# Diffusion backbone on one core: v of the gated-MLP quads in a slot of its own, normalised by ScalarE, and even gated blocks made one quad later

## The chip, the core and the metric

The kernel runs on 1 core of one Trainium2 chip. The core has TensorE (PE: matmuls; its weight loads have rows of their own, PEld), VectorE (DVE), ScalarE (ACT), GpSimd (POOL) and SyncE (SP), whose queue issues nearly all DMA transfers here. The metric is the device time of one execution in microseconds; of several runs the median is taken. The profile shown comes from one profiled execution.

## The reference, cut to what matters

Two layers are computed on 512 latent tokens of width 1024: a retention layer, then a gated MLP (gMLP) layer with spatial mixing over chunks of 128 tokens, and a final RMS norm. The change is in the gMLP layer:

```python
def gmlp_chunk_mixer(h, w_in, vnorm_g, w_s, b_s, w_out):
    u = h @ w_in[:, :GM_WIDTH]
    v = (h @ w_in[:, GM_WIDTH:2 * GM_WIDTH]).astype(F32)
    z = h @ w_in[:, 2 * GM_WIDTH:]
    v = v - jnp.mean(v, axis=-1, keepdims=True)
    v = v * lax.rsqrt(jnp.mean(v * v, axis=-1, keepdims=True) + NORM_EPS) * vnorm_g.astype(F32)
    b, l, w = v.shape
    vg = v.reshape(b, l // CHUNK, CHUNK, GM_GROUPS, w // GM_GROUPS)
    mixed = jnp.einsum('gij,bnjgc->bnigc', w_s.astype(F32), vg) + b_s.astype(F32).T[:, :, None]
    y = u * mixed.reshape(b, l, w).astype(u.dtype)
    return (y * jax.nn.silu(z)) @ w_out
```

GM_WIDTH is 2048 and GM_GROUPS is 8, so a group has 256 channels.

## The kernel before, in words

**Number format.** A float32 product is made of three matmuls in the format fp32r: each operand is split into a high part (a cast, by ScalarE) and a low part (the operand less its high part, by VectorE). `split` issues these two; `mm3` issues the three matmuls. A weight block of 128x1024 is fetched from DRAM by two DMAs of 256 KB into one of 7 slots (the tiles named `raw`), and its high and low parts stand in one of 4 `hl` tiles, used in turn. Those are freed when TensorE has finished the product that reads them.

**Quads.** Eight quads of u and z follow each other (`for i in range(UZ)`, quads 0 to 7). In quad i, 256 columns of u and z are computed for all 512 tokens, by Strassen's scheme for a 2x2 block product with 7 products instead of 8. The products stand in the order B11, T1, T2, B21, T3, B22, T4. The weights of T1 to T4 are combinations of two raw blocks, which VectorE makes in place (rows `raw<-raw`): T1 and T2 both rework the block 11, so the sum for T2 can be made only when the low part of T1 exists. Each product is 24 matmuls of 256 columns (rows `pst<-oA,hl` and `pst<-oS,hl`; the oA and oS tiles are the activations' splits). B11, T2, T3 and T4 add into one PSUM bank, x; B21 has a bank y, T1 and B22 a bank z. Between products that add into x, ScalarE copies its state out (rows `snap<-pst`: after B11, T1 and T2), and VectorE adds such copies to a bank to get the blocks 11, 12 and 22 of the result (rows `snap<-pst,snap`). The block 21 stays in x. Left blocks are the even feature block 2i, right ones the odd feature block 2i+1 (columns: 256 wide, u in the first half and z in the second).

**The spatial product and the gate.** v has been computed before the quads and spilled to DRAM. `load_vt(i)` fetches the 512 KB of v for group i in two halves and normalises each with two `tensor_scalar` on VectorE (v minus mean, times the reciprocal deviation). It is called after T2 of quad i-1, from a pool of eleven 2 KB buffers (`t2`). Behind B22 of quad i stand 16 matmuls of 128 columns (rows `pst<-wsT,vt`), 8 for each of two PSUM banks, `pms[0]` and `pms[1]`. T4 closes the quad. `gate_f(f, ...)` makes the gated block y of feature block f: SiLU of z by ScalarE (rows `yz`), then VectorE: one `scalar_tensor_tensor` from the spatial bank, two products with u, one with the SiLU, and the split of the result (rows `ya`; `yb` and `yc` are the same for other tiles). The odd block's gate stands after the spatial product, the even block's after T4.

**The output projection.** After quads 2, 4, 6 and at the end, `out1` multiplies four finished feature blocks with the output weights (rows `pst<-hl,ya`, 512 columns each): after quad 2 those of quads 0 and 1, and so on. Quads 1, 2, 4 and 6 follow another quad directly; quads 3, 5 and 7 follow an `out1`.

**What sets the order.** TensorE's order is that of the text. In this part of the kernel VectorE, ScalarE and SyncE are not held to the text: the framework's scheduler orders each of these queues when the program is built, and each engine then runs its own queue strictly in that order. All tile sizes and addresses are laid out ahead (`lay`); the slots `w0` to `w6` are the raw slots here, and `w7` and `la` are free in the quads of the kernel before.

Most rows of the profile bear line 54, the helper through which instructions are issued, so work is told apart by tile names.

Of the kernel before, what the change touches and what calls it, by code (L numbers as in the profile page):

```python
# [9 lines left out]
AF = mybir.ActivationFunctionType  # L10
ALU = mybir.AluOpType
AX = mybir.AxisListType

P = 128
# [5 lines left out]
NT = SEQ // P  # L20
# [6 lines left out]
HS = 256  # L27
# [40 lines left out]
def hybrid_kernel(ctx, tc, xT_d, cT_d, cv_d, sv_d, rows_d, ada0_d, adag_d, w_d, rope_d, dec_d, ws_d, id_d, out_d):  # L68
    nc = tc.nc
    pe, act, dve, sp = (Queue(tc, e) for e in (nc.tensor, nc.scalar, nc.vector, nc.sync))  # L70
# [11 lines left out]
    def st(shape, tag, dt=F32, bufs=1, name=None):  # L82
        return sb.tile(shape, dt, tag=tag, name=name or tag, bufs=bufs)

    T2 = 11
# [32 lines left out]
    def t2(name, shape=(P, 512), dt=F32):  # L118
        return st(list(shape), "t2", dt, bufs=T2, name=name)

    def pt(shape=(P, 512), tag="ps"):
        return ps.tile(list(shape), F32, tag=tag, name="pst", bufs=6 if tag == "ps" else 2)

    mm = pe.matmul
# [19 lines left out]
    def load(dst, src):  # L144
        sp.dma_start(dst, src)
# [147 lines left out]
    UZ = 8  # L293
# [781 lines left out]
    vt_d = [dram.tile([P, NT, HS], F32, name=f"vt{i}", tag=f"vt{i}") for i in range(8)]  # L1075
# [137 lines left out]
    wsT = st([P, D], "dec", name="wsT")  # L1213
# [4 lines left out]
    mv = st([P, NT, 2], "mv")  # L1218
    for t in range(NT):
        dve.bn_aggr(mv[:, t, :], bns[:, t, :, :])  # L1220
    rv = st([P, NT], "rv")
    act.activation(rv, mv[:, :, 1], AF.Sqrt, bias=eps, scale=1.0)
    dve.reciprocal(rv, rv)

    o1 = [st([P, D], f"s{t}", name="o1") for t in range(NT)]
    ya = st([P, 4, 2, SEQ], "hc", F32R, name="ya")
# [4 lines left out]
    def yf(f):  # L1231
        return ys[f % 6] if f < 14 else late_y[f - 14]

    def out1(p, hfs=range(2)):
        for hf in hfs:
            ws = [Q.get() for _ in range(2)]
            for t in range(NT):
                last = (p, hf, t) == (3, 1, NT - 1)
                for c in range(2 if last else 1):
                    n = HS if last else 512  # L1240
                    pr = pt((P, n))
                    for k in range(4):
                        y = yf(4 * p + k)
                        w = ws[k // 2][:, :, k % 2 * 512 + c * n:k % 2 * 512 + c * n + n]
                        mm3(pr, (y[:, 0, t * P:t * P + P], y[:, 1, t * P:t * P + P]), (w[:, 0, :], w[:, 1, :]), k == 0, k == 3)
                    if last:
                        last_part(t, c, pr)
                    else:
                        drain(p, t, hf, pr)
# [55 lines left out]
    vts = {}  # L1305

    def load_vt(i):
        vts[i] = []
        for th in range(2):
            v = t2("vt", (P, 2, HS))  # L1310
            load(v, vt_d[i][:, 2 * th:2 * th + 2, :])
            for t in range(2):
                n = 2 * th + t
                dve.tensor_scalar(v[:, t, :], v[:, t, :], mv[:, n, 0:1], rv[:, n:n + 1], ALU.subtract, ALU.mult)
            vts[i].append(v)

    def gate_f(f, pm, mine):

        g = f // 2
        a = t2("ya")  # L1320
        z1 = t2("yz")
        bb = bsb[:, g * P:g * P + P].unsqueeze(1).to_broadcast([P, NT, P])
        for th in range(2):
            act.activation(z1[:, th * HS:th * HS + HS], mine[th][:, HS:], AF.Silu)
        dve.scalar_tensor_tensor(a.rearrange("p (n i) -> p n i", n=NT), pm.rearrange("p (n i) -> p n i", n=NT),
                                 vg[:, f:f + 1], bb, ALU.mult, ALU.add)
        for th in range(2):
            h = a[:, th * HS:th * HS + HS]
            dve.tensor_tensor(h, mine[th][:, 0:HS], h, ALU.mult)
        dve.tensor_tensor(a, a, z1, ALU.mult)  # L1330
        y = yf(f)
        split((y[:, 0, :], y[:, 1, :]), a)

    load_vt(0)
    for i in range(UZ):
        got, pms = {}, {}
        prod = Product(features, got.__setitem__)
        for name in SINGLE:
            prod.run(name, Q.get())
            if name == "T2" and i < UZ - 1:  # L1340
                load_vt(i + 1)
            if name == "T2" and i == UZ - 1:
                pair_y = st([P, 2, 2, SEQ], "oA11", F32R, name="yc")
                late_y += [pair_y[:, j] for j in range(2)]
            if name == "B22":
                for s in range(2):
                    pm = pms[s] = pt()
                    for n in range(NT):
                        mm(pm[:, n * P:n * P + P], vts[i][n // 2][:, n % 2, s * P:s * P + P], wsT[:, i * P:i * P + P], start=True, stop=True)
                gate_f(2 * i + 1, pms[1], {0: got["12"], 1: got["22"]})  # L1350
        gate_f(2 * i, pms[0], {0: got["11"], 1: got["21"]})
        if i and i % 2 == 0:
            out1(i // 2 - 1, range(2 if i < UZ - 2 else 1))
    out1(2, (1,))
    out1(3)


# [108 lines left out]
```

## Time and profile before

| what | value |
|---|---|
| median of 3 runs | 899.59 us (899.02 to 902.96) |
| time of the profiled execution | 897.46 us |
| its span, first to last instruction | 895.7 us |
| busy: PE, PEld | 874.6 us (98%), 830.3 us (93%) |
| busy: DVE, ACT, POOL | 720.5 us (80%), 446.4 us (50%), 51.6 us (6%) |
| mean granted TensorE clock | 0.998 |
| the quads and output projections | from 625.72 us to the end |

The profiled execution took 897.46 us, 1.76 us more than its span, and stands 2.13 us below the median of the runs. A row of the timeline gives the start, the length, the engine, the operation with its output and inputs, the number of instructions merged into it, and in brackets the idle time of the engine just before, with what ended it. TensorE is busy nearly all the time, so a change can only win where the timeline shows TensorE or its weight loads idle, or where its matmuls follow each other more slowly than elsewhere.

### The profile page before, as it was taken

The page shows a single profiled execution, that of the slowest core. Times are in us where ns is not written, and L with a number is a line of the kernel's source. Part 1 is how long each engine was busy: PE and PEld are TensorE (multiplying, and loading weights), DVE is VectorE, ACT ScalarE, POOL GpSimd, SP SyncE. Part 2 cuts the span into 40 slices and gives each one's busy share as a digit, 9 for nine tenths or more (in the row PEclk, how much of TensorE's full clock was granted, in tenths as well). Part 3 has the DMA queues.
Part 4 walks back from the last instruction along what each step waited for, and adds up shares of the span by engine and source line. Part 5 has one row for each costly group of instructions (what it writes and reads, how often), then busy time and mean ns, then how long its engine had stood idle before and what let it go on. Part 6 is the DMA issues. An engine that isn't in the chain of part 4 may idle for free.

```text
span 895.7 us, 16947 instructions
## 1 busy us (share of the span) xinstructions
PE 874.6 (98%) x6884; PEld 830.3 (93%) x6884; DVE 720.5 (80%) x1027; ACT 446.4 (50%) x685; POOL 51.6 (6%) x88
## 2 busy tenths in 40 slices
PE   8999999999999999999999999999999999999997
PEld 6899999999999999998989898999999899899986
DVE  2689978698789876888677669999889578779995
ACT  5465644434545436626263448744545445245334
POOL 0001201101102011000000001011000000000000
PEclk9999999999999999999999999999999999999999
DMA  9933977566576468758254611626335135136212
GB/s 334 405 125 107 297 233 259 163 182 232 173 235 231 140 201 305 260 162 267 76 173 133 197 51 60 199 108 223 131 118 168 45 119 178 35 119 212 60 59 95
DMA packets 76638, 153.81 MB, mean 172 GB/s; under 512 B 7824, under 2 KB 34576, under 8 KB 76560
## 3 DMA queue, kind: packets, MB, share of 16 engines
q1 hardware_dynamic: 69696, 130.70, 44.9%
q0 software_dynamic: 6720, 22.03, 6.4%
q8 instruction: 54, 0.88, 0.4%
q14 instruction: 24, 0.20, 0.1%
q10 hardware_dynamic: 144, 0.01, 0.0%
HBM read 128.58 MB, written 24.12 MB: 170 GB/s over the span
## 4 chain that ended last, share of the span: by engine, by line
PE 70%; DVE 17%; ACT 5%; DMA 4%; issue 3%; SPq 1%; DVEq 0%; ACTq 0%
PE pst L54 70%; DVE hl L54 6%; DVE raw L54 3%; DMA raw<-in_w_dram 2%; DVE ya L54 2%; ACT hl L54 1%; DMA xq<-in_xT_dram 1%; DVE snap L54 1%; DMA vt<-vt 1%; DVE f L54 1%; DVE pf L54 1%; ACT junk L54 1%; SPq L54 1%; DVE oS L54 1%; ACT f L54 1%
## 5 line engine op out<-in xcount | busy, mean ns | idle before, releaser
L54 DVE TENSOR_TENSOR hl<-raw,hl 128x1024 fp32r<-128x1024 f32 x195 | 236.0, 1218 | 62.8 <-ACT hl L54 62.5
L54 ACT CAST hl<-raw 128x1024 fp32r<-128x1024 f32 x195 | 203.9, 1050 | 125.4 <-PE pst L54 63.0
L54 PE MATMUL pst<-oS,hl 128*128 128x256 f32 x1104 | 134.0, 279 | 5.1 <-DVE hl L54 4.5
L54 PEld LDWEIGHTS pst<-oS,hl 128*128 128x128 f32 x1104 | 129.9, 188 | 7.5 <-ACT ya L54 4.2
L54 PE MATMUL pst<-hl,oS 128*128 128x256 f32 x1152 | 134.0, 277 | 2.1 <-DVE hl L54 1.9
L54 PEld LDWEIGHTS pst<-hl,oS 128*128 128x128 f32 x1152 | 132.0, 188 | 3.6 <-DVE hl L54 2.4
L54 PE MATMUL pst<-oA,hl 128*128 128x256 f32 x936 | 117.3, 281 | 0.2
L54 PEld LDWEIGHTS pst<-oA,hl 128*128 128x128 f32 x936 | 111.9, 189 | 2.8 <-issue 1.3
L54 DVE TENSOR_TENSOR raw<-raw 128x1024 f32<-128x1024 f32 x92 | 111.3, 1217 | 1.2 <-DMA raw<-in_w_dram 0.5
L54 ACT COPY snap<-pst 128x512 f32<-128x512 f32 x92 | 53.8, 586 | 95.2 <-PE pst L54 95.0
L54 PE MATMUL pst<-hl,oA 128*128 128x256 f32 x816 | 97.1, 277 | 0.4 <-DVE snap L54 0.4
L54 PEld LDWEIGHTS pst<-hl,oA 128*128 128x128 f32 x816 | 94.6, 188 | 0.8 <-issue 0.6
L54 PE MATMUL pst<-og,hl 128*128 128x256 f32 x768 | 92.6, 281 | 0.0
L54 PEld LDWEIGHTS pst<-og,hl 128*128 128x128 f32 x768 | 90.5, 189 | 0.9 <-issue 0.5
L54 PE MATMUL pst<-v,ph 128*128 128x512 f32 x192 | 60.1, 395 | 0.0
L54 PE MATMUL pst<-hl,ya 128*128 128x512 f32 (+1 forms) x246 | 59.6, 388 | 0.0
L54 PEld LDWEIGHTS pst<-hl,ya 128*128 128x128 f32 x246 | 45.4, 188 | 9.8
L54 DVE TENSOR_TENSOR snap<-pst,snap 128x512 f32<-128x512 f32 x69 | 47.1, 683 | 3.5 <-PE pst L54 3.3
L54 ACT CAST ph<-pf 128x512 fp32r<-128x512 f32 x24 | 14.9, 621 | 67.4 <-DVE pf L54 66.9
L54 PE MATMUL pst<-hl,hc 128*128 128x256 f32 x384 | 46.1, 276 | 0.0
L54 PEld LDWEIGHTS pst<-hl,hc 128*128 128x128 f32 x384 | 44.7, 188 | 0.0
L54 PEld LDWEIGHTS pst<-v,ph 128*128 128x128 f32 x192 | 36.2, 188 | 7.3
(176 smaller groups left out, 992.8 us busy)
## 6 DMA issues: line engine op xcount, KB each, us to landing
raw<-in_w_dram SPq DMA_DIRECT2D x224, 256.0 KB, 4.6
bg<-in_adag_dram SPq DMA_DIRECT2D x32, 512.0 KB, 4.3
ada_w<-in_ada_dram SPq DMA_DIRECT2D x16, 512.0 KB, 8.8
raw<-in_w_dram SPq DMA_DIRECT2D x16, 512.0 KB, 4.3
bg<-in_dec_dram SPq DMA_DIRECT2D x12, 512.0 KB, 4.5
v<-snap POOLq DMA_DIRECT2D x16, 256.0 KB, 5.3
z<-snap POOLq DMA_DIRECT2D x16, 256.0 KB, 4.8
v<-v SPq DMA_DIRECT2D x8, 512.0 KB, 4.3
```

What stands on the lines that cost most here:

```text
L54: made = op(*args, **kw)
```

## The change

- A third small tile, `nm`, holds minus the mean times the reciprocal deviation.
- The 512 KB of v for a group come in one DMA into `w7`, a slot of their own with one buffer. The load for quad i+1 is issued after the spatial product of quad i has read the slot (in the text, behind B22 of quad i; before, behind T2 of quad i).
- The normalisation is four ScalarE activations (Identity with a scale and a bias per partition) in the text behind T2 of the quad that uses v, in place of four VectorE instructions behind T2 of the quad before.
- The even block's gate of quad i is put into the list `behind` and issued by `settle()`: in the text behind T2 of the next quad, or, where an `out1` follows, after its first two weight blocks; in quad 7 at once. So it moves into another quad for quads 0, 1, 3 and 5 (and for quad 2, 4 and 6 a little into the `out1`).

```diff
+    nm = st([P, NT], "la", name="nm")
+    dve.scalar_tensor_tensor(nm, mv[:, :, 0], -1.0, rv, ALU.mult, ALU.mult)
...
             ws = [Q.get() for _ in range(2)]
+            settle()
             for t in range(NT):
...
     def load_vt(i):
-        vts[i] = []
-        for th in range(2):
-            v = t2("vt", (P, 2, HS))
-            load(v, vt_d[i][:, 2 * th:2 * th + 2, :])
-            for t in range(2):
-                n = 2 * th + t
-                dve.tensor_scalar(v[:, t, :], v[:, t, :], mv[:, n, 0:1], rv[:, n:n + 1], ALU.subtract, ALU.mult)
-            vts[i].append(v)
+        v = vts[i] = st([P, NT, HS], "w7", name="vt")
+        load(v, vt_d[i])
+
+    def norm_vt(i):
+        for n in range(NT):
+            v = vts[i][:, n, :]
+            act.activation(v, v, AF.Identity, bias=nm[:, n:n + 1], scale=rv[:, n:n + 1])
...
     load_vt(0)
+    behind = []
+
+    def settle():
+        while behind:
+            behind.pop(0)()
+
     for i in range(UZ):
...
-            if name == "T2" and i < UZ - 1:
-                load_vt(i + 1)
+            if name == "T2":
+                norm_vt(i)
+                settle()
...
                     for n in range(NT):
-                        mm(pm[:, n * P:n * P + P], vts[i][n // 2][:, n % 2, s * P:s * P + P], wsT[:, i * P:i * P + P], start=True, stop=True)
+                        mm(pm[:, n * P:n * P + P], vts[i][:, n, s * P:s * P + P], wsT[:, i * P:i * P + P], start=True, stop=True)
+                if i < UZ - 1:
+                    load_vt(i + 1)
                 gate_f(2 * i + 1, pms[1], {0: got["12"], 1: got["22"]})
-        gate_f(2 * i, pms[0], {0: got["11"], 1: got["21"]})
+        behind.append(lambda i=i, pm=pms[0], mine={0: got["11"], 1: got["21"]}: gate_f(2 * i, pm, mine))
+        if i == UZ - 1:
+            settle()
```

What this does to the queues is seen where quad 0 passes into quad 1. TensorE's queue keeps its order. On VectorE, before (`hl_7740` is the low part of T1 of quad 1, `hl_7778` that of T2; `ya_7729` is the odd gated block of quad 0, `ya_7767` the even one):

```order
L54 TENSOR_TENSOR hl_7740<-raw_7295,hl_7740 128x1024
L54 SCALAR_TENSOR_TENSOR ya_7729<-pst_7724,sv_128,bsb_7493 128x512
L54 SCALAR_TENSOR_TENSOR ya_7767<-pst_7719,sv_128,bsb_7493 128x512
L54 TENSOR_TENSOR ya_7729<-snap_7614,ya_7729 128x256
L54 TENSOR_TENSOR ya_7729<-snap_7581,ya_7729 128x256
L54 TENSOR_TENSOR ya_7767<-snap_7551,ya_7767 128x256
L54 TENSOR_TENSOR ya_7729<-ya_7729,yz_7730 128x512
L54 TENSOR_TENSOR ya_7767<-pst_7526,ya_7767 128x256
L54 TENSOR_TENSOR raw_7295<-raw_7333,raw_7295 128x1024
L54 TENSOR_TENSOR ya_7511<-ya_7729,ya_7511 128x512
L54 TENSOR_TENSOR ya_7767<-ya_7767,yz_7768 128x512
L54 TENSOR_TENSOR hl_7778<-raw_7295,hl_7778 128x1024
```

and with the change (`hl_7734` is the low part of T1, `hl_7762` that of T2, `ya_7723` the odd gated block):

```order
L54 TENSOR_TENSOR hl_7734<-raw_7295,hl_7734 128x1024
L54 TENSOR_TENSOR snap_7610<-pst_7552,snap_7610 128x512
L54 TENSOR_TENSOR raw_7295<-raw_7333,raw_7295 128x1024
L54 SCALAR_TENSOR_TENSOR ya_7723<-pst_7716,sv_128,bsb_7493 128x512
L54 TENSOR_TENSOR ya_7723<-snap_7610,ya_7723 128x256
L54 TENSOR_TENSOR ya_7723<-snap_7577,ya_7723 128x256
L54 TENSOR_TENSOR hl_7762<-raw_7295,hl_7762 128x1024
```

Nine gate instructions and the sum for T2 stood between the low parts of T1 and T2; three gate instructions stand there now, the even block's gate comes later.

On ScalarE at the same place, before (`hl_7778` is T2, `hl_7839` T3 of quad 1; `snap_7806` is the copy of bank x after B11):

```order
L54 CAST hl_7808<-raw_7587 128x1024
L54 CAST ya_7511<-ya_7729 128x512
L54 CAST hl_7778<-raw_7295 128x1024
L54 COPY snap_7806<-pst_7781 128x512
L54 CAST ya_7511<-ya_7767 128x512
L54 CAST hl_7839<-raw_7330 128x1024
```

and with the change (`hl_7762` is T2, `hl_7823` T3; `snap_7790` is the copy after B11, `vt_7721` is v for quad 1):

```order
L54 CAST hl_7762<-raw_7295 128x1024
L54 CAST hl_7792<-raw_7583 128x1024
L54 ACTIVATE vt_7721<-vt_7721,nm_7507,rv_7504 128x256
L54 CAST ya_7513<-ya_7723 128x512
L54 ACTIVATE vt_7721<-vt_7721,nm_7507,rv_7504 128x256 x2
L54 COPY snap_7790<-pst_7765 128x512
L54 CAST hl_7823<-raw_7330 128x1024
L54 ACTIVATE vt_7721<-vt_7721,nm_7507,rv_7504 128x256
```

The cast for T2 moved ahead, and three of the four normalisations, which wait for the DMA, stand ahead of the copy after B11.

## The prediction

> **What bounds the kernel now.** I read the page first, busy times and the chain that ended last:
>
> ```profile
> PE 874.6 (98%) x6884; PEld 830.3 (93%) x6884; DVE 720.5 (80%) x1027; ACT 446.4 (50%) x685; POOL 51.6 (6%) x88
> ...
> PE 70%; DVE 17%; ACT 5%; DMA 4%; issue 3%; SPq 1%; DVEq 0%; ACTq 0%
> ```
>
> TensorE is the bound. VectorE's 17% of the chain says that in places TensorE waits for it or nearly does. So the next view is who waited, weight loads and then matmuls, between 640 and 860 us, where the quads stand:
>
> ```profile
> PEld pst L54 <- ACT ya L54: 4.2, 3, 2.0
> PEld pst L54 <- ACT yb L54: 1.0, 1, 1.0
> ```
>
> ```profile
> PE pst L54 <- DVE hl L54: 4.5, 4, 1.8
> ```
>
> All that can be won there is these few waits. The timeline of the weight loads places them: T2 of quads 1, 2, 4 and 6, the four that directly follow another quad, and T4 of quad 4.
>
> ```profile
> 654.38 2.82 PEld L54 LDWEIGHTS pst<-oS,hl 128*128 128x128 f32 x24 [1.78 <-ACT ya L54]
> ...
> 677.57 2.82 PEld L54 LDWEIGHTS pst<-oS,hl 128*128 128x128 f32 x24 [1.95 <-ACT ya L54]
> ...
> 742.58 2.80 PEld L54 LDWEIGHTS pst<-oS,hl 128*128 128x128 f32 x24 [0.42 <-ACT ya L54]
> ...
> 755.56 2.81 PEld L54 LDWEIGHTS pst<-oA,hl 128*128 128x128 f32 x24 [0.23 <-DVE snap L54]
> ...
> 808.11 2.89 PEld L54 LDWEIGHTS pst<-oS,hl 128*128 128x128 f32 x24 [1.01 <-ACT yb L54]
> ```
>
> Together 5.39 us. What T2 of quad 1 waits for is seen on VectorE:
>
> ```profile
> 640.24 1.43 DVE L54 TENSOR_SCALAR vt<-vt,mv,rv 128x256 f32<-128x256 f32 x4 [2.33 <-DMA vt<-vt]
> ...
> 646.32 1.22 DVE L54 TENSOR_TENSOR hl<-raw,hl 128x1024 fp32r<-128x1024 f32 x1
> 647.45 1.40 DVE L54 SCALAR_TENSOR_TENSOR ya<-pst,sv,bsb 128x512 f32<-128x512 f32 x2
> 648.77 1.08 DVE L54 TENSOR_TENSOR ya<-snap,ya 128x256 f32<-128x256 f32 x3
> ...
> 650.71 1.21 DVE L54 TENSOR_TENSOR raw<-raw 128x1024 f32<-128x1024 f32 x1
> ...
> 652.45 0.68 DVE L54 TENSOR_TENSOR ya<-ya,yz 128x512 f32<-128x512 f32 x1
> 653.05 1.22 DVE L54 TENSOR_TENSOR hl<-raw,hl 128x1024 fp32r<-128x1024 f32 x1
> ```
>
> VectorE stands 2.33 us idle for the DMA of v, normalises, and then is busy without a gap to the low part of T2 at 653.05, because the gates of both feature blocks stand ahead of it. TensorE was due sooner:
>
> ```profile
> 644.38 5.70 PE L54 MATMUL pst<-oA,hl 128*128 128x256 f32 x48
> 649.91 2.88 PE L54 MATMUL pst<-oS,hl 128*128 128x256 f32 x24
> 654.41 2.98 PE L54 MATMUL pst<-oS,hl 128*128 128x256 f32 x24 [1.62 <-DVE hl L54]
> 657.24 2.88 PE L54 MATMUL pst<-oA,hl 128*128 128x256 f32 x24
> 659.96 5.60 PE L54 MATMUL pst<-oS,hl 128*128 128x256 f32 x48
> ...
> 672.83 2.99 PE L54 MATMUL pst<-oS,hl 128*128 128x256 f32 x24
> 677.60 2.98 PE L54 MATMUL pst<-oS,hl 128*128 128x256 f32 x24 [1.78 <-DVE hl L54]
> 680.42 2.88 PE L54 MATMUL pst<-oA,hl 128*128 128x256 f32 x24
> ...
> 811.04 2.99 PE L54 MATMUL pst<-oA,hl 128*128 128x256 f32 x24
> 813.87 5.81 PE L54 MATMUL pst<-oS,hl 128*128 128x256 f32 x48
> ```
>
> Two things are to be seen. T2 of quad 1 was due when T1 had issued, at 649.91 + 2.72 = 652.63. And a product of 24 matmuls has two paces: from 657.24 to 659.96 it takes 2.72 us, from 811.04 to 813.87 2.83 us. A merged row of 24 is 2.88 long at the quick pace and 2.99 at the slow one. Quad 2 enters T1 at the slow pace (672.83), waits, and leaves at the quick one (680.42); quad 6 leaves its wait slow. The pace holds from product to product until something interrupts.
>
> **The change part by part.**
>
> *Low part of T2 earlier (the gain).* With the change VectorE has, between the low parts of T1 and T2, one sum into a copy, the sum for T2 and three gate instructions. Counting from the end of the spatial product, about 644.4, which the gate needs: 0.70 (half of the 1.40), two of 0.36 (1.08 for three), and the low part, 1.22, so the low part is done near 647.1, or near 647.8 if the sum for T2 (1.21) ends only at 645.2. Due is 652.63. The wait of 1.78 goes, with some 4.8 us to spare. In quad 2, which holds the deferred gate of quad 0, more stands behind the spatial product of quad 1: the low part of T1 (1.22), the first gate instruction (0.70), the sum (1.21), two gate products (0.72), one with the SiLU (0.68) and the low part of T2 (1.22), 5.75 us; due is T2 8.58 us after it: 652.63 - 644.38 = 8.25 as in quad 1, and three products at the slow pace, each 2.83 - 2.72 = 0.11 more. Quads 4 and 6 have the order of quad 1 again, and go the same way. The 0.23 before T4 of quad 4 is a copy on VectorE that stood behind the normalisation; that is gone from this queue. Sum: -5.39 us.
>
> *Normalisation from VectorE to ScalarE.*
>
> ```profile
> L54 DVE TENSOR_SCALAR vt<-vt,mv,rv 128x256 f32<-128x256 f32 x32 | 11.6, 408 | 13.2 <-DMA vt<-vt 13.2
> L54 DVE RECIPROCAL rv<-rv 128x4 f32<-128x4 f32 x1 | 0.2, 171 | 0.0
> ```
>
> ```profile
> L54 ACT ACTIVATE f<-f,sh,gs x16: 586/590/602, 538.8 to 577.2; 128x256 f32<-128x256 f32 x16
> ```
>
> ```profile
> 538.92 2.47 ACT f L54 x5
> ```
>
> ```profile
> L54 ACT CAST hl<-raw 128x1024 fp32r<-128x1024 f32 x71 | 74.3, 1050 | 57.0 <-PE pst L54 34.1 <-DVE raw L54 19.2 <-issue 3.7
> L54 ACT COPY snap<-pst 128x512 f32<-128x512 f32 x26 | 15.3, 587 | 20.4 <-PE pst L54 20.3
> ...
> L54 ACT CAST ya<-ya 128x512 fp32r<-128x512 f32 x10 | 6.2, 621 | 6.9 <-DVE ya L54 6.8
> ```
>
> VectorE loses 32 instructions (11.6 us busy, and the 13.2 us it stood for their DMA); they count in the gain above and not again. It gets one `nm` of 128x4 elements, near the 0.17 us of the reciprocal, once. ScalarE gets 32 activations. The nearest row is an Identity with scale and bias tiles of the same size: 0.59 us each, 0.49 from one to the next (2.47 for five). That is about 2.06 us a quad; ScalarE is half idle, so in itself it costs nothing, except where it is queued ahead of something due.
>
> *The new wait on ScalarE.* Three of four activations stand ahead of the copy of bank x after B11, in quads 1, 4 and 6; T2 adds to that bank and must wait for the copy. From the landing of v: 0.59, a cast of the gate 0.62, two more activations 0.49 + 0.59, the copy 0.59: 2.88 us. T2 is due 652.63 - 644.38 = 8.25 us after the spatial product at the quick pace, 8.58 at the slow pace of quads 4 and 6. So v must land within 5.4 us (quad 1) or 5.7 us (quads 4, 6) of the spatial product. In quad 2 only two activations stand ahead (0.49 + 0.59 + 0.59 = 1.67): 6.9 us.
>
> ```profile
> DMA to landing us min/median/max: 2.3/4.3/6.2
> ```
>
> ```profile
> vt<-vt SPq DMA_DIRECT2D x16, 256.0 KB, 4.7
> ```
>
> ```profile
> v<-v SPq DMA_DIRECT2D x8, 512.0 KB, 4.3
> ...
> ada_w<-in_ada_dram SPq DMA_DIRECT2D x16, 512.0 KB, 8.8
> ```
>
> The loads of v take 2.3 to 6.2 us now, 4.7 in the quads; the nearest single transfer of 512 KB from a spill takes 4.3. I take 4.3 to 4.7, which leaves 0.7 us or more: cost 0. Bounds: below, 0 (a sooner landing wins nothing, T2 is not waiting then); above, 6.2 us, which costs 0.8 + 0.5 + 0.5 = 1.8 us. Behind quads 2, 4 and 6 an `out1` follows, so v of quads 3, 5 and 7 has some 20 us more.
>
> *What queues behind the load of v on SyncE.* The load now waits for the spatial product; behind it stand raw blocks for two quads ahead and, after quad 6, the four loads of the residual. The raw blocks next in line need slots that T3 of the following quad frees, later than the load is issued. Cost 0; the residual is due only when the first projection block has been drained.
>
> *Quad 0.* Here the activations wait for `nm`, behind the reciprocal:
>
> ```profile
> 630.55 1.19 DVE L54 TENSOR_TENSOR raw<-raw 128x1024 f32<-128x1024 f32 x1
> ```
>
> ```profile
> 637.02 5.82 PE L54 MATMUL pst<-oS,hl 128*128 128x256 f32 x48
> ```
>
> `nm` is ready near 631.9; four activations, two copies (0.59 each) and a cast (1.05) then end near 636.3, and T3, which needs the second copy, starts at 637.02. Cost 0, with 0.7 us left.
>
> *Held longer.* Bank x and a spatial bank stay in use until T3 of the next quad; there are six such banks and a quad takes three, so they are asked for again a whole quad later. Cost 0.
>
> *Pace (given back).* Without the waits, quads 2 and 4 stay at the slow pace in which they enter: B21, T3 and B22 at 2.83 in place of 2.72, 6 x 0.11 = 0.66 us. Quad 1 was quick and stays so; its T2, slow after the wait (657.24 - 654.41 = 2.83), wins 0.11. Quad 6 was slow throughout.
>
> Sum: -5.39 + 0.66 - 0.11 = -4.84 us. The profiled execution of 897.46 us becomes 892.6; against the median of 899.59, which stands 2.13 higher, 894.75 us. Half a per cent, about what a measurement of this kernel can tell from no change, is 4.50 us: the bound is 895.09, and the forecast lies just beyond it.
>
> By the matmul rows alone the idle time would be 4.5 us and not 5.39, so the forecast 895.6. The Trainium skill's page Perfetto Trace Analysis (Identifying the Most-Contended Engine) calls matmul busy time a poor measure since pipelined matmuls look smaller, and prefers the weight loads. The starts decide for the weight loads here: 654.41 - 652.63 is 1.78.
>
> **The rivals.**
>
> *One pace.* If the pace is not carried over, nothing is given back: 899.59 - 5.39 = 894.2. For it: three of the four waits, and each `out1`, left TensorE quick. Against: quad 6 stayed slow for four products. The Trainium skill's page TensorE: Matmul & The Clock Gate (Wait — 56ns, not 53.3ns?) has one warm spacing, N / 2.4 GHz + 2.5 ns, which by an estimate from it is 2.62 us for 24 matmuls of 256 whatever came before; by that rule this rival holds. The trace shows neither 2.62 nor one value.
>
> *Slow also in quad 1.* The spatial product leaves TensorE slow after quad 1 (672.83); after quad 0 it did not (649.91). If it now does, six products of quad 1 lose 0.11: 894.75 + 0.66 = 895.4.
>
> *v lands late.* The wait moves from VectorE's low part to ScalarE's copy. At a landing of 6.2 us, 894.75 + 1.8 = 896.6. For each us more all of the four quads lose one: 4 L - (5.4 + 5.7 + 5.7 + 6.9) eats the 4.84 at L = 7.1 us, and from there the kernel is slower than before. At 8.8, the landing of the crowded loads at the start, 11.5 us are lost and the time is 906.3. Against: the raw blocks ahead are fetched by then, so v has the DMA engines to itself. For: one transfer in place of two, asked for later, and ScalarE's strict order.
>
> **How the numbers follow.** The forecast as summed 0.47, its own range 893.7 to 895.7; one pace 0.10; slow also in quad 1 0.12; v late but under 7.1 us 0.15; v later than that, with what else a rebuilt order may do to a queue, 0.16. Faster by over 0.5%: 0.40 of the first case and all of one pace, 0.50. Within: 0.07 of the first, 0.12 and 0.15, and 0.01 of the last, 0.35. Slower 0.15. The range goes from 893.0 (one pace, and runs reach 0.6 below their median: 899.02 against 899.59) to 900.5, just past the point where late v eats the gain; above it some 0.13 is left out.
>
> **What would show it.** Right: no idle before the weight loads of T2 in quads 1, 2, 4 and 6; VectorE without `vt` rows and without waits for DMA; merged rows of 2.99 through quads 2 and 4. Wrong: weight loads that wait for `snap` on ScalarE, `vt` activations idle for the DMA past 5.4 us after the spatial product, or a new wait in an `out1`.

## The result and the profile after

| | median | runs | ratio to before, 95% interval |
|---|---|---|---|
| before | 901.23 us | 899.02 to 902.96 | |
| changed | 896.61 us | 893.55 to 898.68 | 0.9951 (0.9937 to 0.9965) |

The changed kernel is 4.6 us faster by the medians, about half a per cent. Its profiled execution, however, took 898.68 us, 1.22 us more than that of before (897.46). Two things hide in that number, and they have to be kept apart: what the quads gained, and what the work ahead of them did.

The page of the changed kernel, busy times and the chain that ended last:

```profile
PE 881.9 (98%) x6884; PEld 839.2 (94%) x6884; DVE 712.7 (79%) x996; ACT 461.2 (51%) x717; POOL 51.5 (6%) x88
...
PE 88%; DVE 5%; ACT 3%; DMA 2%; issue 1%; SPq 1%; DVEq 0%; ACTq 0%
```

VectorE's share of the chain fell from 17% to 5%. The view of waits of the weight loads from 640 to 900 us, which named 5.2 us for the gate's casts before, has no row left; this is its whole answer:

```profile
core 0 of [0], span 896.9 us
engine line waited for: us in total, times, longest us
```

TensorE's timeline of the changed kernel from the spatial product of quad 0 on:

```profile
644.04 5.82 PE L54 MATMUL pst<-oS,hl 128*128 128x256 f32 x48
649.70 1.95 PE L54 MATMUL pst<-wsT,vt 128*128 128x128 f32 x16
651.40 5.70 PE L54 MATMUL pst<-oA,hl 128*128 128x256 f32 x48
656.94 5.60 PE L54 MATMUL pst<-oS,hl 128*128 128x256 f32 x48
...
670.54 1.95 PE L54 MATMUL pst<-wsT,vt 128*128 128x128 f32 x16
672.24 5.90 PE L54 MATMUL pst<-oA,hl 128*128 128x256 f32 x48
677.98 5.82 PE L54 MATMUL pst<-oS,hl 128*128 128x256 f32 x48
683.63 2.99 PE L54 MATMUL pst<-oA,hl 128*128 128x256 f32 x24
686.46 5.82 PE L54 MATMUL pst<-oS,hl 128*128 128x256 f32 x48
692.11 1.95 PE L54 MATMUL pst<-wsT,vt 128*128 128x128 f32 x16
693.82 2.98 PE L54 MATMUL pst<-oA,hl 128*128 128x256 f32 x24
696.64 22.14 PE L54 MATMUL pst<-hl,ya 128*128 128x512 f32 x96
718.61 2.91 PE L54 MATMUL pst<-oA,hl 128*128 128x256 f32 x24
```

T1 and T2 stand merged in one row (5.60 or 5.82 for 48), since nothing comes between them. Quad 1 is quick (5.60), quad 2 is slow throughout (5.82, 2.99, 5.82), and T4 of quad 2 at 693.82 is quick again.

VectorE and then ScalarE in quad 1:

```profile
652.33 0.74 DVE L54 SCALAR_TENSOR_TENSOR ya<-pst,sv,bsb 128x512 f32<-128x512 f32 x1
653.11 0.76 DVE L54 TENSOR_TENSOR ya<-snap,ya 128x256 f32<-128x256 f32 x2
653.78 1.22 DVE L54 TENSOR_TENSOR hl<-raw,hl 128x1024 fp32r<-128x1024 f32 x1
```

```profile
655.42 0.59 ACT L54 ACTIVATE vt<-vt,nm,rv 128x256 f32<-128x256 f32 x1
655.92 0.60 ACT L54 CAST ya<-ya 128x512 fp32r<-128x512 f32 x1
656.43 1.09 ACT L54 ACTIVATE vt<-vt,nm,rv 128x256 f32<-128x256 f32 x2
657.43 0.56 ACT L54 COPY snap<-pst 128x512 f32<-128x512 f32 x1
```

The low part of T2 (653.78) is done at 655.0; T2 starts at 656.94 + 2.72 = 659.66, so 4.7 us are to spare. The copy of bank x is done at 658.0, 1.7 us ahead of T2. In quad 2, for which the prediction had reckoned the most room, it is less: the copy there is done at 679.51 and T2 starts at 677.98 + 2.83 = 680.81, 1.3 us later. In quads 4 and 6 it is 1.9 us.

What the work ahead of the quads did is seen in the first long stretch of products. The first row is before, the second the changed kernel, the same product in code that the change doesn't touch:

```profile
112.11 2.88 PE L54 MATMUL pst<-hl,hc 128*128 128x256 f32 x24
```

```profile
113.77 2.99 PE L54 MATMUL pst<-hl,hc 128*128 128x256 f32 x24
```

The profiled execution of before ran this stretch of 36 products at the quick pace (with two short stops), that of the changed kernel at the slow one. Ahead of the first spatial matmul 1648 starts of 256-column matmuls follow each other at the slow pace in before and 3150 in the changed kernel; at 117.8 against 113.3 ns each that is 6.7 us, and the first spatial matmul starts 7.0 us later (649.70 against 642.68). So from here on every profile is read from the start of its first spatial matmul to the start of its last matmul, "the stretch": 246.4 us before, 240.85 us with the change, 5.5 us less.

### The profile page after: what moved, and what is told of

It is laid out like the page before. It is cut to its first block, busy times and chain, and to the rows that moved or that the text cites. A ratio compares the mean times of both kernels' runs of the same rounds, so it can differ in the third digit from the quotient of the medians.

```text
span 896.9 us, 16938 instructions
## 1 busy us (share of the span) xinstructions
PE 881.9 (98%) x6884; PEld 839.2 (94%) x6884; DVE 712.7 (79%) x996; ACT 461.2 (51%) x717; POOL 51.5 (6%) x88
## 4 chain that ended last, share of the span: by engine, by line
PE 88%; DVE 5%; ACT 3%; DMA 2%; issue 1%; SPq 1%; DVEq 0%; ACTq 0%
PE pst L54 88%; DVE hl L54 2%; DMA xq<-in_xT_dram 1%; DVE raw L54 1%; DMA raw<-in_w_dram 1%; ACT hl L54 1%; ACT junk L54 1%; SPq L54 1%; ACT f L54 1%; ACT oA L54 0%; DVE ada_a L54 0%; DVE pf L54 0%; DVE pl L54 0%; DVE o L54 0%; DVE f L54 0%
## 5 line engine op out<-in xcount | busy, mean ns | idle before, releaser
L54 PE MATMUL pst<-hl,oS 128*128 128x256 f32 x1152 | 138.6, 282 | 2.1 <-DVE hl L54 1.9
L54 PEld LDWEIGHTS pst<-hl,oS 128*128 128x128 f32 x1152 | 136.6, 190 | 3.4 <-DVE hl L54 2.1
L54 PE MATMUL pst<-hl,oA 128*128 128x256 f32 x816 | 99.3, 280 | 0.0
L54 PEld LDWEIGHTS pst<-hl,oA 128*128 128x128 f32 x816 | 97.2, 189 | 0.1
```

The lines of the kernel that those rows point to most:

```text
L54: made = op(*args, **kw)
```

## The experiments

| kernel | ratio to before, 95% interval | stretch, us | weight loads' waits in it, us |
|---|---|---|---|
| before, first and second profile | | 246.4, 244.5 | 5.4, 2.3 |
| changed, first | 0.9951 (0.9937 to 0.9965) | 240.85 | 0 |
| changed, second | 0.9961 (0.9946 to 0.9975) | 240.85 | 0 |
| changed, third | 0.9946 (0.9930 to 0.9961) | 240.85 | 0 |
| deferred gates alone | 1.0072 (1.0048 to 1.0095) | 251.9 | 8.6 |
| v alone | 0.9947 (0.9923 to 0.9971) | 242.0 | 0.5 |
| slot and late load alone | 0.9946 (0.9929 to 0.9963) | 240.85 | 0 |
| changed, normalised by VectorE | 0.9929 (0.9905 to 0.9953) | 240.86 | 0 |
| changed, late v | single run | 244.8 | 4.1 |
| changed, order on ScalarE alone | single run | 240.85 | 0 |
| changed, spatial product split | 0.9939 (0.9918 to 0.9961) | 244.8, begins sooner | 1.0 |
| changed, a 512-column matmul in quads 2, 4, 6 | 0.9923 (0.9903 to 0.9943) | 240.3 | 0 |
| changed, such matmuls at 13 places | 0.9993 (0.9979 to 1.0006) | 241.2 | 0 |

**Is the difference ahead of the quads the execution's or the kernel's?** Both kernels again, unchanged.

> The changed kernel once more, for its profile. Theory (its first profiled execution was longer than that of before, 898.68 against 897.46 us, only because the unchanged work ahead of the quads ran more of its matmuls at the slow pace; that part differs from execution to execution): the first spatial matmul starts somewhere from 641 to 651 us, and from there to the last matmul it takes 240.9 us again, within 0.5 us. Rival (the change itself makes the work ahead of the quads slower, through another layout or order): the first spatial matmul starts at 649.7 us within 1 us again.

> The changed kernel beside the two others, on the same chip. Both theories: 240.85 us within 0.3 from the first spatial matmul to the last, ratio to before 0.993 to 0.997; what differs from execution to execution is the number of slow intervals ahead of the quads, in long stretches that are slow or quick as a whole. Against it: another time in the quads, or single slow products in between.

> The kernel before once more, for its profile. Theory (the pace ahead of the quads is a matter of the execution, the waits in the quads are one of the kernel): the start of the first spatial matmul moves by some us from the 642.7 of the first profile, while the stretch from there to the last matmul is 246.4 us within 0.7 and the weight loads of T2 in quads 1, 2, 4 and 6 wait 5 to 5.5 us together again. Rival (the pace belongs to the program): 642.7 within 0.5 us again.

The changed kernel's first spatial matmul started at 649.7, 648.5 and 646.1 us in its three profiles, and the stretch took 240.85 us each time. In the third the 36 products switched pace in the middle. So the start is a matter of the execution. (In all three quad 0 was entered at the slow pace.) The second profile of before began at 648.0, and there the expectation failed in its other half: the waits were not 5 to 5.5 us again.

```profile
658.90 2.89 PEld L54 LDWEIGHTS pst<-oS,hl 128*128 128x128 f32 x24 [0.70 <-ACT ya L54]
...
681.00 2.81 PEld L54 LDWEIGHTS pst<-oS,hl 128*128 128x128 f32 x24 [0.46 <-ACT ya L54]
...
746.68 2.89 PEld L54 LDWEIGHTS pst<-oS,hl 128*128 128x128 f32 x24 [1.11 <-ACT ya L54]
```

T2 of quads 1, 2 and 4 waited 2.27 us, that of quad 6 not at all. The stall is a race between VectorE and TensorE. In this execution TensorE stayed slow through quad 1, where it had been quick in the first profile, so T2 was due later, and VectorE stood 1.60 us for v in place of 2.33; how much each of the two did isn't told apart. The gain in the stretch is 5.5 us against the first profile of before and 3.6 us against the second. The three comparisons by medians give 4.6, 2.8 and 4.6 us.

**Which part carries the gain?** First the deferred gates without the new v:

```diff
+            if name == "T2":
+                settle()
...
-        gate_f(2 * i, pms[0], {0: got["11"], 1: got["21"]})
+        behind.append(lambda i=i, pm=pms[0], mine={0: got["11"], 1: got["21"]}: gate_f(2 * i, pm, mine))
```

> One part alone: the even gates are made in the next quad, v is fetched and normalised as before (two halves, by VectorE, behind T2 of the quad ahead). Theory (the low part of T2 was late by 0.4 to 2 us, and either part alone takes more than that out of VectorE's queue in front of it): VectorE still stands idle for the DMA of v and normalises it in front of T1's low part, but five gate instructions (about 3 us) leave the way to T2's low part. In quad 1 it is then done near 651.3 against a due time of 652.6; the weight loads of T2 in quads 1, 2, 4 and 6 wait 0 to 0.5 us together in place of 5.16, and from the first spatial matmul to the last one it takes 241 to 242 us (before 246.4, after 240.9). Ratio to before 0.994 to 0.996. Rival A (v is what held T2 up): 2.5 us or more of the waits stay, the stretch takes 243.5 us or more, ratio 0.997 or above. Rival B (the two parts are worth about half each): half of the 5.4 us, 243 to 244 us.

It is slower than before, 1.0072, and the stretch grew to 251.9 us. The theory's 241 to 242 us and rival B's 243 to 244 were wrong. Rival A's bounds hold (2.5 us or more of waits, 243.5 us or more, ratio 0.997 or above), but it too expected waits that stay, not new ones. VectorE in quad 1:

```profile
669.91 0.73 DVE L54 TENSOR_SCALAR vt<-vt,mv,rv 128x256 f32<-128x256 f32 x2 [3.23 <-DMA vt<-vt]
670.56 0.42 DVE L54 TENSOR_TENSOR ya<-snap,ya 128x256 f32<-128x256 f32 x1
670.89 0.73 DVE L54 TENSOR_SCALAR vt<-vt,mv,rv 128x256 f32<-128x256 f32 x2
671.54 0.42 DVE L54 TENSOR_TENSOR ya<-pst,ya 128x256 f32<-128x256 f32 x1
```

VectorE comes to the normalisation with nothing else left ahead of it and stands 3.23 us for the DMA of v (4.80 us in quad 4; 18.5 us in eight stands in all, against 13.2 before). The deferred even gate of quad 0 (the `ya<-snap,ya` and `ya<-pst,ya` rows) is now queued behind that stand. What was idle time ahead of the even gate before is now idle time followed by it, and T1 and T2 of quad 2 (1.56 and 1.74 us), T4 of quads 4 and 6 (1.47 and 0.62) and T2 of quad 7 (3.21) wait. That the deferral alone costs time is shown by the run; that the stand is the way by which it does is read from quad 1 and wasn't followed for the later waits.

Then the new v without the deferred gates:

> The other part alone: v in the slot of its own, loaded late and normalised by ScalarE; the gates of both blocks are made where they were. Theory (either part is enough): the low part of T2 loses the idle time for the DMA (2.33 us in quad 1) and four normalisations (4 x 0.36 = 1.45 us) in front of it, so it comes 3.8 us sooner, at 650.5 in place of 654.3 against a due time of 652.6; the T2 waits are 0 to 0.5 us together, the stretch from the first spatial matmul to the last 241 to 242 us, ratio 0.994 to 0.996. Rival A (the even gate held T2 up): 2.5 us or more stay, 243.5 us or more, ratio 0.997 or above. Rival B (half each): 243 to 244 us.

Its diff is that of the change without `behind` and `settle`. The ratio is 0.9947 and the waits of T2 in quads 1, 2, 4 and 6 are gone; only T2 of quad 7 waited, 0.55 us. The rest of its 1.2 us over the changed kernel is mostly the first output projection, of which more below. So v carries the gain and the deferral alone costs time; they are not two halves of it. Then the two halves of v. VectorE gets its normalisation back, all else as in the change:

```diff
-            act.activation(v, v, AF.Identity, bias=nm[:, n:n + 1], scale=rv[:, n:n + 1])
+            dve.tensor_scalar(v, v, mv[:, n, 0:1], rv[:, n:n + 1], ALU.subtract, ALU.mult)
```

> The changed kernel with the normalisation given back to VectorE (the subtract and multiply of the kernel before, in the quad that uses v); slot, late load and deferred gates stay. Theory (what must leave VectorE's way is the wait for the DMA, the 1.5 us of work a quad matters little): v lands some 3.3 us after its issue behind the spatial product, VectorE reaches it about a microsecond early, and the low part of T2 in quad 1 is done near 656.5 on the clock of the first profile after, against a due time of 659.7. No weight load of T2 waits over 0.3 us, the stretch from the first spatial matmul to the last takes 240.8 to 241.6 us, ratio to before 0.994 to 0.997. Rival (the normalisation has to leave VectorE): the stand for the DMA and the 1.5 us come in front of the low parts, T2 waits 2 us or more in all, the stretch takes 243 us or more, ratio 0.998 or above.

and the same with the gates where they were, so that only the slot, the time of the load and the place of the normalisation differ from before:

> The kernel before with the slot of its own and the late load alone: v is normalised by VectorE in the quad that uses it, and the gates of both blocks are made where they were. Theory (what held T2 up was VectorE standing for the DMA of v ahead of its own due work; the load behind the spatial product and the normalisation behind the low part of T2 take that away, and neither ScalarE nor the deferred gates are needed): behind the spatial product of quad 0 VectorE has the two first gate instructions (1.40), three gate products (1.08), one with the SiLU (0.68), one more (0.36) and the low part of T2 (1.22), so it is ready about 5 us behind it against the 8.25 at which T2 is due. Waits of weight loads in the quads under 1 us in all, from the first spatial matmul to the last 241 to 242 us, ratio 0.993 to 0.997. Rival (the move to ScalarE or the deferral carries the gain): 2.5 us of waits or more stay, 243.5 us or more, ratio 0.997 or above.

No weight load of the quads waits in either, and the stretch is 240.86 and 240.85 us, that of the change to a hundredth of a microsecond. VectorE of the second in quad 1:

```profile
654.96 0.41 DVE L54 TENSOR_TENSOR ya<-pst,ya 128x256 f32<-128x256 f32 x1
655.30 1.21 DVE L54 TENSOR_TENSOR hl<-raw,hl 128x1024 fp32r<-128x1024 f32 x1
...
660.51 1.37 DVE L54 TENSOR_SCALAR vt<-vt,mv,rv 128x256 f32<-128x256 f32 x4
```

All gate instructions still stand ahead of the low part of T2 (655.30), and it is done at 656.5, 2.9 us early: the spatial product ended at 651.1 there, and T2 is due 8.25 us behind it. The normalisation comes after it. The slot of its own, the late load and the normalisation in the quad that uses v, which the scheduler then puts behind the low part, are the whole gain. Neither the move to ScalarE nor the deferral is needed for it. No run parts these three from each other. By an estimate from the rows of before, the stand alone would have been enough in quad 1: it took 2.33 us of a queue that then ran without a gap, more than the wait of 1.78, while the four normalisations took 1.35 (640.24 to 641.59).

**How late may v be?** The load was issued twice in a row for every quad but quad 0, and on ScalarE three normalisations were kept ahead of the copy after B11; a control has that order with one load.

```diff
         load(v, vt_d[i])
+        if i:
+            load(v, vt_d[i])
...
+            if early:
+                norm_vt(i, range(3))
+                act.pinned = True
+            prod.run(name, w)
+            act.pinned = False
```

> The changed kernel with v fetched twice in a row into its slot (the second DMA waits for the first), so that it lands later, and on ScalarE three of its normalisations kept ahead of the copy after B11 in quads 1, 2, 4 and 6. Landing of the second: about 6.6 us behind the issue of the first, some 7 us behind the spatial product. Theory (from the landing it takes 0.49 + 0.49 + 0.59 and the copy, 0.59, 2.16 us in all, until T2 may start, due 8.25 us behind the spatial product at the quick pace and 8.58 at the slow one): each T2 of these quads waits the landing less 6.1 us (6.4 slow), 0.5 to 1.0 us, 2 to 4 us in all, released by ScalarE's copy; each further microsecond would cost four. Rival (late v is covered by spare time that the sum did not see): under 0.5 us of waits in all.

> The kernel of the late v, with v fetched once as in the changed kernel; the order on ScalarE stays (three normalisations ahead of the copy after B11 in quads 1, 2, 4 and 6). Theory (in the kernel with late v it was the landing that made T2 wait, by the landing behind the spatial product less 6.1 us, or 6.4 at the slow pace): v lands some 5.5 us behind the end of the spatial product or sooner, no T2 waits over 0.2 us, and the stretch from the first spatial matmul to the last takes 240.8 to 241.1 us. Rival (the order alone made the waits): the weight loads of T2 in quads 1, 2, 4 and 6 wait 2 us or more in all, released by ScalarE's copy.

Weight loads of the kernel with late v:

```profile
658.34 2.89 PEld L54 LDWEIGHTS pst<-oS,hl 128*128 128x128 f32 x24 [0.65 <-ACT snap L54]
...
680.89 2.82 PEld L54 LDWEIGHTS pst<-oS,hl 128*128 128x128 f32 x24 [1.21 <-ACT snap L54]
...
746.00 2.81 PEld L54 LDWEIGHTS pst<-oS,hl 128*128 128x128 f32 x24 [0.52 <-ACT snap L54]
...
812.00 2.81 PEld L54 LDWEIGHTS pst<-oS,hl 128*128 128x128 f32 x24 [1.69 <-ACT snap L54]
```

and its ScalarE in quad 6:

```profile
809.90 1.58 ACT L54 ACTIVATE vt<-vt,nm,rv 128x256 f32<-128x256 f32 x3 [1.07 <-DMA vt<-vt]
811.39 1.04 ACT L54 COPY snap<-pst 128x512 f32<-128x512 f32 x2
```

The first normalisation starts 6.76, 7.33, 6.93 and 8.11 us behind the four spatial products (809.90 less 801.79 in quad 6). Less 6.1 at the quick pace (quads 1 and 2) or 6.4 at the slow one (4 and 6) that is 0.66, 1.23, 0.53 and 1.71; measured are 0.65, 1.21, 0.52 and 1.69. The control waits nowhere; with one load the scheduler also put one cast behind the copy that stands ahead of the normalisations with two. So the rival in which the wait moves to ScalarE's copy has the price that the prediction gave it, a microsecond a quad for each microsecond. In quads 2 and 6 ScalarE stood for the DMA itself. In quads 1 and 4 the normalisation came straight behind a cast that the scheduler had put ahead of it and that waited for TensorE; how much of those two waits is the landing and how much that cast isn't told apart.

**What is the pace?** The prediction let it pass from product to product. The spatial product was split, 8 matmuls behind T3 and 8 behind B22:

```diff
-            if name == "B22":
-                for s in range(2):
+            if name in ("T3", "B22"):
+                for s in ((0,) if name == "T3" else (1,)):
```

> The changed kernel with the 16 spatial matmuls in two parts: the 8 of the even block behind T3, the 8 of the odd block behind B22. Theory (a stretch of 128-column matmuls turns the pace of the 256-column ones over, slow to quick and quick to slow, however many they are): each quad is turned twice, only B22 stands at the other pace. If quad 0 is entered quick, all rows of the quads are 2.88 (24) or 5.60 (48) but for B22, about 190 intervals are slow in place of 546 and the stretch from the first spatial matmul of the kernel to the last shrinks by about 1.6 us beside the 2.8 us by which it begins sooner; if it is entered slow, quads 0 to 2 stay slow but for B22 up to the output projection and the rest is quick, about 430 slow intervals, 0.5 us gained. Rival A (16 are needed, or it is the place and not the kind of matmul that turns the pace): quads 2, 4 and 6 slow as before, no gain. Rival B (the second stop costs more than it gives): 8 x 0.1 us lost at the extra border.

Quad 3 and T1 and T2 of quad 4 of this kernel:

```profile
728.18 2.88 PE L54 MATMUL pst<-oS,hl 128*128 128x256 f32 x24
730.90 1.05 PE L54 MATMUL pst<-wsT,vt 128*128 128x128 f32 x8
731.71 3.07 PE L54 MATMUL pst<-oS,hl 128*128 128x256 f32 x24
734.62 1.06 PE L54 MATMUL pst<-wsT,vt 128*128 128x128 f32 x8
735.43 5.70 PE L54 MATMUL pst<-oA,hl 128*128 128x256 f32 x48
740.98 5.60 PE L54 MATMUL pst<-oS,hl 128*128 128x256 f32 x48
```

T3 is quick, B22 slow, the rest quick: each run of eight turned the pace over. Quad 0 was entered slow and the turns came as the theory has them for that case (460 slow intervals, 430 expected). But nothing was gained, against the 0.5 us expected. The product behind each run takes some 0.1 us longer than its pace (2.91 for B22 at 731.71), which the second run of each quad adds eight times in all, and T4 of quad 7 waited 0.6 us for VectorE. The stretch begins one product sooner, B22 of quad 0 with 2.82 us; set against that it is 1.1 us longer.

Then one additional matmul of 512 columns ahead of B11 in quads 2, 4 and 6, and after it the same at 13 places of the whole kernel:

```diff
+            if reset and name == "B11":
+                mm(bank, w[:, 0, 0:P], A["A11"][:, 0, 0:2, :], start=True, stop=True, skip_group_check=True)
```

> The changed kernel with one additional matmul of 512 columns ahead of B11 in quads 2, 4 and 6, into the bank that B11 then overwrites; nothing reads its result. Theory (the pace is a state of TensorE that a 512-column matmul sets to quick, as every output projection left it quick): the six products up to B22 of these quads go from 2.83 to 2.72 us where they were slow, 3 x 6 x 0.11 = 2.0 us gained, against 3 x 0.22 = 0.66 us for the matmuls and up to 3 x 0.11 for T4, which the spatial product then leaves slow: the stretch from the first spatial matmul to the last 239.8 to 240.2 us in place of 240.85. Rival (one such matmul doesn't set it, or the pace belongs to the place in the program): quads 2, 4 and 6 stay at 2.99 a row, the stretch takes 241.5 us.

> The changed kernel with the additional 512-column matmul ahead of B11 at 13 places: the first of the two paired projections at the start, six of the nine later ones, the two pairs of v, and quads 1, 2, 4 and 6. Each writes into the bank that B11 then overwrites; nothing reads its result. Theory (such a matmul sets the quick pace from whatever pace is there, and the pace then holds): the 36 products from about 60 to 162 us are quick in every execution (864 slow intervals less, 3.8 us), the three kq projections too (some 620 less, 2.7 us), the products of v for the most part (100 to 640 slow intervals now, about 1.2 us on the mean), quads 2, 4 and 6 as with the three alone (0.5 us after their cost); the ten other matmuls cost 10 x 0.22 = 2.2 us. Together some 6 us: median about 891 us, ratio to before 0.987 to 0.991. Rival A (the first stretch is slow for another reason, such as its operands or the transfers at that time): 1.5 to 2.5 us, ratio 0.991 to 0.994. Rival B (the additional matmul turns a quick pace slow, or the scheduler's new order makes waits): no gain over the changed kernel.

First the kernel with three matmuls, in quad 2; then the one with 13, in quad 1:

```profile
670.29 6.03 PE L54 MATMUL pst<-oA,hl 128*128 128x256 f32 x49
676.15 5.60 PE L54 MATMUL pst<-oS,hl 128*128 128x256 f32 x48
```

```profile
652.18 6.03 PE L54 MATMUL pst<-oA,hl 128*128 128x256 f32 x49
658.04 5.82 PE L54 MATMUL pst<-oS,hl 128*128 128x256 f32 x48
```

A row of 49 is T4, the additional matmul and B11. With three of them quads 2, 4 and 6 became quick, 176 slow intervals in place of 546, and the stretch 0.53 us shorter, 240.3 us where 239.8 to 240.2 were expected. It looked much as the theory said, but all three had been entered slow. With 13 the theory fell: in quad 1 the intervals ahead of the additional matmul are 113.3 ns, those behind it 117.7. The very first place looks the same, entered at 113 ns and left slow, but it shows nothing: the changed kernel, which has no such matmul there, is entered at 113 ns and left slow as well. First the kernel with 13, then the changed one:

```profile
59.87 0.39 PE L54 MATMUL pst<-oA,hl 128*128 128x512 f32 x1
60.09 2.99 PE L54 MATMUL pst<-hl,oA 128*128 128x256 f32 x24
```

```profile
60.06 2.99 PE L54 MATMUL pst<-hl,oA 128*128 128x256 f32 x24
```

So each place has to be held against the same place without the matmul. Six of the 13 are clean: those at 161.9 and 593.7 us and the four in the quads, where the other profiles keep their pace (with one exception, at 161.9 us in the first profile of before). There the matmul turned the pace every time, three times from quick to slow (593.7 us, quads 1 and 2) and three times from slow to quick (161.9 us, quads 4 and 6). With the three of the first kernel that is nine of nine: it doesn't set the quick pace, it turns the pace over. At six other places the pace changes without the matmul too in all or nearly all other profiles, so they don't tell, and at one the pace behind it can't be read. The 13 matmuls at 0.22 us are 2.9 us of the 3.7 by which the median of this kernel lies above the changed kernel's on the same chip; the rest wasn't traced. The version with three has the shortest stretch; its median, 895.17 us, isn't told apart from the changed kernel's by the intervals.

## Why the prediction was right, point by point

**The waits of T2 (-5.39).** Right for the execution from which they were read, all five gone: by the starts of the matmuls the products with the waits take 5.58 us less, 0.11 of it in T2 of quad 1. That 0.11 the prediction read as the slow pace; the intervals show a slow start behind the stop, about five long ones and then 113 ns again. That this was one execution was not weighed: in another the waits were 2.27 us. The gain to be had was 2.3 to 5.4 us of waits, and the forecast took the upper end.

**Why T2 had been late.** Half right. The stand for v's DMA and the nine instructions ahead of the low part were added up as one gain, as if each part of the change took its own share. The runs show that the stand, with the normalisation behind it, is what counted. With it gone the even gate may stay where it was, with it in place the deferral makes things worse. The list of VectorE's instructions between the spatial product and the low part was right to 0.1 us (4.7 us to spare, forecast 4.8), but it didn't tell which of them had to go.

**Normalisation on ScalarE (0).** Right: 0.595 us each, busy time from 446.4 to 461.2 us, no wait of TensorE through it. In quad 0 it waited 1.2 us for `nm`, and this cost nothing, as forecast: the copy that T3 needs was done at 642.4 us and T3 started with 1.6 us left.

**The new wait on ScalarE (0).** Right, with more room than assumed. The landing of v's loads in the changed kernel, of those issued from 630 to 860 us:

```profile
DMA to landing us min/median/max: 3.1/3.3/4.5
```

The median is 3.3 us where 4.3 to 4.7 was taken. The price past the limit, a microsecond a quad for each microsecond, was confirmed by quads 2 and 6 of the kernel with late v.

**Pace given back (+0.66).** Right: quads 2, 4 and 6 ran slow throughout, and B21, T3 and B22 of quads 2 and 4 took 0.64 us more by their starts.

**What the sum lacked.** T4 of quads 2 and 6 and the first output projection. T4 of quad 2 and the projection before:

```profile
690.28 3.07 PE L54 MATMUL pst<-oA,hl 128*128 128x256 f32 x24
693.19 22.56 PE L54 MATMUL pst<-hl,ya 128*128 128x512 f32 x96
```

Together they took 25.31 us before (690.28 to 715.59) and 24.79 with the change (693.82 to 718.61). T4 of quad 2 is quick with the change and was slow before; in every profile with a slow T4 there the two take 25.31, with a quick one 24.79 to 24.82. So the 512-column matmuls of that projection run at another pace too, worth 0.43 us; T4 itself wins 0.09, and that of quad 6 as much. By the starts this gives -5.58 + 0.64 - 0.18 - 0.43 = -5.55 of the 5.52 measured, so nothing of size is left over.

**The rivals.** *One pace* is out: the two paces are in all 14 profiles, and quads 2, 4 and 6 kept the slow one up to the next spatial product. The Trainium skill's page TensorE: Matmul & The Clock Gate (Wait — 56ns, not 53.3ns?) would have 256 / 2.4 + 2.5, an estimate of 109.2 ns from one 256-column matmul to the next; measured are 113.3 and 117.8. That figure is for matmuls back to back, and here each has a weight load beside it (6884 of either), so that both are longer decides nothing; but the rule has one value, which leaves nothing to turn over, and the trace has two. *Slow also in quad 1* didn't happen in the changed kernel, but it does when quad 0 is entered quick, as the kernel with v alone was. *v lands late* didn't happen; its price for each microsecond was right. By the matmul rows alone the forecast would have been 895.6; by the starts the waits gave 5.58 us, so the 5.39 of the weight loads were nearer than the 4.5 of the matmul rows. The Trainium skill's page Perfetto Trace Analysis (Identifying the Most-Contended Engine) calls the busy share of the matmuls no good measure of how close a kernel is to its roofline and has that of the weight loads read instead, beside the share of peak FLOPs reached; it speaks of busy shares and not of single waits, but this trace points the same way.

**The total.** Forecast were 4.84 us less; measured are 4.6 by the medians of the first comparison and 2.8 and 4.6 in two more. In per cent that is 0.54 forecast and 0.49 measured (0.35 to 0.63), so on which side of half a per cent the change lies isn't decided. The median of 896.61 us lies above the forecast's own range of 893.7 to 895.7, since the median of before came out 1.64 us above the 899.59 from which it was reckoned. That the two differences stand so near is in part luck: the waits were those of one execution, and the 0.6 us of T4 and the projection, which the sum didn't have, happen to make good what the pace took.

## What to carry to other kernels

When a wait on a strict queue is to be removed, ask which instruction the engine stands at and not only how many stand ahead of the late one: here a load issued later, so that its consumer could be queued behind the urgent work, was the whole gain, and moving work out of the way without that made the kernel slower. Where a matmul-bound kernel's runs spread by half a per cent, read two profiles of the same kernel before a stall is priced, and compare from a fixed point in the program, since what lies ahead of the change may differ by more than the change is worth. Try an effect from both starting states: a matmul that seemed to set a pace only turned it over. And look at the same place in a profile without it, since some places turn the pace by themselves.

## What was not expected of the hardware

- 256-column fp32r matmuls follow each other in one of two paces, 113.3 or 117.8 ns, at a granted clock of 0.995 to 0.999 in all profiles. A pace holds for up to 36 products, in the same code quick in one execution and slow in another: 98.26 and 101.76 us for that stretch in the two profiles of before. Most of the spread of a kernel's runs may follow from it, which wasn't measured run by run.
- The spatial product's run of 128-column matmuls turns it over, whether 8 or 16: 96 times of 96 in the kernels with v in its own slot, and 16 of 24 in those with v in two pool buffers (both profiles of before and the deferred gates alone). Not every run of 128-column matmuls does: ahead of the quads, eight with the identity (`pst<-ident,acc`, 526.62 us in the first profile of before) have a slow product on either side, 3.08 and 3.07 us. Why the buffers should matter is open, and so is the cause of the two paces.
- One 512-column matmul takes 0.22 us and turned it over at all nine places where the pace is otherwise kept. The output projections after quads 2, 4 and 6, with 48 or 96 such matmuls, left TensorE quick in 41 of 42 cases, whichever pace T4 had; the exception is the one after quad 4 in the second profile of before. No short insert that was tried sets one pace from both.
